# Input quarters of a seven-product projection loaded once and held, four pairs begun before the sums, recurrence units placed earlier

## The chip, the cores and the metric

One Trainium2 chip, one of its cores. The metric is the device time of one execution in microseconds (us); the number that counts is the median over runs. The engines are TensorE (PE in the profile, its weight loads PEld), VectorE (DVE), ScalarE (ACT), GpSimd (POOL) and SyncE (SP), which here only issues loads.

## The reference

A decoder layer over 2048 tokens of width 1024 in float32. One input projection feeds two groups: a gated linear recurrence (HGRN2, four heads of 128) and sliding-window attention with sinks (eight query heads, two key heads). Their gated outputs go through one output projection, and LayerNorm ends the layer:

```python
h = jnp.einsum('btd,de->bte', h_res, w_in[layer])          # 1024 -> 3328 columns
hq, hf, hi, hg, aq, ak, av, ag = jnp.split(h, IN_SPLITS, axis=-1)
f = lb + (1.0 - lb) * jax.nn.sigmoid(hf)
o_h = hgrn2_chunk(silu(hq), 1.0 - f, hi, log(f))           # S_t = diag(f_t) S_{t-1} + (1-f_t) i_t^T
o_h = rms_norm(o_h) * hg_norm_w * silu(hg)
o_a = swa_with_sinks(partial_rope(aq), partial_rope(ak), av, sinks[layer]) * silu(ag)
out = jnp.einsum('btd,de->bte', jnp.concatenate([o_h, o_a], -1), w_out[layer])
z = DN_ALPHA * h_res + out                                  # then LayerNorm with ln_g, ln_b
```

## The kernel before

**Projection.** The 26 column tiles of 128 are taken in 13 pairs (`PAIRS`, L38), the tokens in two super-blocks of 1024. A super-block and a pair make a 2 x 2 block product, which is done with seven products instead of eight. The blocks of x are a11, a12 (first 512 tokens, lower and upper half of the 1024 inputs), a21, a22 (second 512 tokens). Besides a11, a12 and a22 the products use four sums: s1 = a21 + a22, s2 = s1 - a11, s3 = a11 - a21, s4 = a12 - s2. Each of these operands is four tiles of 128 x 512 and is called a quarter here where it is a block of x. The product numbers are those of the weights: 1 (with a11), 2 (a12), 6 (s2), 5 (s1), 7 (s3), 3 (s4), 4 (a22); the weights 4 to 7 are sums, too (t1, t2 in `Weights.make`, L267), made in the first super-block, stored in DRAM (kw) and loaded again in the second.
Every operand is split into a high and a low part, the high one by ScalarE (L184), the low one by VectorE (L185). A product is then 12 matmuls of 512 columns (`product`, L323). Three accumulators hold the results in PSUM: px, py and pz, from a pool `mm_ps` of six banks that attention and recurrence use as well.

**Order.** The 91 products of a super-block are its slots (L761 on). The slots begin with products 1 and 2 of the first `GROUP` pairs, three before the change, because these need no sums; after them each pair's others follow in the order 6, 5, 7, 3, 4. `SuperBlock` (L207) makes the operands: a11 and a12 ahead of the first slot, then `sums` (a21 and a22 loaded, s1, s2, s3), `late` (a12 loaded a second time, s4) and `last` (a22 loaded a second time). The second super-block's are made around slot 91. These second loads, and every weight load, go into one pool of five tiles of 256 KB (`raw_tile`, L153).

**Units.** Attention and recurrence run in pieces between the slots: `attend(j, b)` (L384, seven steps) and `recur(j, b)` (L523, ten steps) for head group j and token block b. The table `units_at` (L777) gives each the slot of its first step and how many slots lie between two steps. Slots past 182 are ticks of the output projection, two for each half of an output tile. Attention queries (qa) and the recurrence's decayed keys and queries (kq) live in a pool of two 1 MB tiles, `q_tile` (L171); decays live in a pool of four e tiles (`e_tile`, L168), where attention has its keys. A recurrence unit multiplies running products of the forget gate (scans L548, L549), a reciprocal (L558) and factors on GpSimd (L560, L561) into kq, transposes the keys on TensorE (kp, L604), and updates a state (L643) for each of four chunks.

**Output projection.** For each of 16 token tiles `out_prepare` (L699) reloads the spilled recurrence and attention outputs (mh, ms), transposes mh, and `out_tile` (L718) does two halves of 24 matmuls (L739 to L741) and the LayerNorm. Its scale lg is kept in two e tiles, its shift lb in the two tmp tiles.

The program is written in this order, and a scheduler places each engine's instructions when the program is built; every engine then runs its own list strictly in order, SP's list of loads included.

Of the kernel before, what the change touches and what calls it, by code (L numbers as in the profile page):

```python
# [10 lines left out]
F32 = mybir.dt.float32  # L11
# [29 lines left out]
GROUP = 3  # L41
# [3 lines left out]
def tile_hybrid_layer(  # L45
# [161 lines left out]
    class SuperBlock:  # L207
# [10 lines left out]

        def a12(self):
            for q in range(4):  # L220
                self.put("a12", q, load_x(self.s, 0, 4 + q, raw_tile, f"r12{q}"))

        def sums(self, q):
            a21, a22 = load_x(self.s, 1, q, t_tile, f"r21{q}"), load_x(self.s, 1, 4 + q, raw_tile, f"p22{q}")
            s1, s2 = raw_tile(f"x{self.s}_s1{q}"), tmp_tile(f"x{self.s}_s2{q}")
            nc.vector.tensor_add(s1, a21, a22)
            nc.vector.tensor_sub(s2, s1, self.r11[q])
            nc.vector.tensor_sub(a21, self.r11[q], a21)
            self.put("s2", q, s2)
# [488 lines left out]
    def out_tile(n, m, made, after):  # L718
        if not lns:
            lg, lbt = [e_tile(f"lg{c}")[:, 0:512] for c in range(2)], [tmp_tile(f"lb{c}") for c in range(2)]  # L720
            for c in range(2):
                nc.sync.dma_start(lg[c], lng[:, c * 512 : (c + 1) * 512].to_broadcast([P, 512]))
                nc.sync.dma_start(lbt[c], lnb[:, c * 512 : (c + 1) * 512].to_broadcast([P, 512]))
            lns.extend([lg, lbt])
# [46 lines left out]
    for g, (s, t, m, w, p) in enumerate(slots):  # L771
# [6 lines left out]
        24: (attend, 0, 0, 3), 38: (attend, 0, 1, 3), 52: (attend, 1, 0, 3), 66: (attend, 1, 1, 3),  # L778
        96: (recur, 0, 0, 2), 106: (recur, 0, 1, 2), 117: (attend, 0, 2, 2), 126: (recur, 1, 0, 2),
        135: (attend, 0, 3, 2), 144: (recur, 1, 1, 2), 153: (attend, 1, 2, 2), 162: (attend, 1, 3, 2),  # L780
# [35 lines left out]
    for g in range(1, LEAD):  # L816
        if g != GROUP:
            make(g)
# [109 lines left out]
```

## Time and profile before

| | |
|---|---|
| median of 3 runs | 1017.3 us (1011.54 to 1021.37) |
| profiled execution, own time | 1012.9 us |
| its span, first to last instruction | 1011.2 us |
| mean granted TensorE clock | 0.939 |
| TensorE busy | 898.4 us (89%) |
| VectorE busy | 644.4 us (64%) |
| ScalarE busy | 462.1 us (46%) |
| GpSimd busy | 268.4 us (27%) |
| moved by DMA | 206.71 MB, mean 204 GB/s |

Busy times are sums over the span of one execution. A matmul's own duration overlaps with the next one's, so the distance between two starts is what one costs. A wait in brackets is idle time of the engine just before an instruction, with the event that ended it. The granted clock is a share of 2.4 GHz.

### The profile page before, as it was taken

To read this page: it belongs to the slowest core of one execution; us is meant where nothing else is said; L and a number is where in the kernel's file an instruction comes from. 1 tells how busy PE (TensorE), PEld (TensorE's weight loads), DVE (VectorE), ACT (ScalarE), POOL (GpSimd) and SP (SyncE) were. 2 spreads that over 40 slices of the span, in tenths; PEclk is the share of its full clock that TensorE was granted. 3 is DMA by queue.
4 is the path that set the end of the run, shared out by engine and by line. 5 is a ranking of instruction groups with operands and counts; after the bars stand their busy time and mean duration, and the time that the engine had idled before them with its cause. 6 is when DMAs were issued, how large, how long until landed. Compare 5 with 4: busy or idle time off the path is not lost.

```text
span 1011.2 us, 14557 instructions
## 1 busy us (share of the span) xinstructions
PE 898.4 (89%) x4542; PEld 714.7 (71%) x4542; DVE 644.4 (64%) x1280; ACT 462.1 (46%) x1236; POOL 268.4 (27%) x444
## 2 busy tenths in 40 slices
PE   8149899999999985899989998999999959699996
PEld 6037687777777764677867886877778747578884
DVE  5956677565665599675556545444886885755554
ACT  5422455444444445365553553554775645433221
POOL 1114333222333102433222222222322222212111
PEclk9669899999999996999999998999999979889998
DMA  6398996767546758778676658556795534234322
GB/s 226 99 308 287 300 330 217 242 211 239 204 177 237 268 188 306 254 252 230 224 209 226 205 185 241 178 141 237 255 311 166 176 101 139 91 110 136 104 84 83
DMA packets 97950, 206.71 MB, mean 204 GB/s; under 512 B 14161, under 2 KB 31697, under 8 KB 97873
## 3 DMA queue, kind: packets, MB, share of 16 engines
q1 hardware_dynamic: 73904, 127.11, 41.2%
q0 software_dynamic: 23680, 78.15, 20.6%
q8 instruction: 36, 0.59, 0.3%
q10 hardware_dynamic: 288, 0.52, 0.1%
q14 instruction: 42, 0.34, 0.1%
HBM read 124.59 MB, written 78.64 MB: 201 GB/s over the span
## 4 chain that ended last, share of the span: by engine, by line
PE 66%; DMA 8%; DVE 7%; ACT 3%; issue 3%; SPq 1%; POOL 1%; DVEq 0%; POOLq 0%; ACTq 0%
PE px L329 7%; PE px L330 7%; PE px L331 7%; PE po L739 5%; PE po L740 5%; PE po L741 5%; PE pz L329 4%; PE pz L331 4%; PE pz L330 4%; PE op L495 2%; DMA r<-proj 2%; PE py L329 2%; PE sp L445 2%; PE py L331 2%; PE py L330 1%
## 5 line engine op out<-in xcount | busy, mean ns | idle before, releaser
L296 POOL DMA_DIRECT2D proj<-s x48 | 26.7, 556 | 141.0 <-DVE s L351 127.6
L346 ACT ACTIVATE s<-px 128x512 f32<-128x512 f32 x52 | 31.0, 597 | 51.3 <-PE px L331 49.2
L558 DVE RECIPROCAL f<-e 128x512 f32<-128x512 f32 x16 | 53.4, 3339 | 0.2
L468 POOL TENSOR_TENSOR wt<-wt,st 128x512 f32<-128x512 f32 x32 | 33.4, 1042 | 56.4 <-DVE st L467 45.5
L459 ACT ACTIVATE wt<-sp,st 128x129 f32<-128x129 f32 x128 | 45.5, 371 | 3.2 <-DVE st L455 2.6
L185 DVE TENSOR_TENSOR w<-w,w 128x512 fp32r<-128x512 f32 x42 | 31.5, 754 | 23.6 <-ACT w L184 23.6
L329 PE MATMUL px<-x_s20h,w 128*128 128x512 f32 x26 | 11.4, 440 | 36.9 <-ACT w L184 35.9
L290 POOL DMA_DIRECT2D kw<-w x52 | 28.2, 543 | 55.7 <-DVE w L185 49.8
L742 DVE SCALAR_TENSOR_TENSOR xr<-xr,po 128x512 f32<-128x512 f32 x32 | 21.9, 683 | 32.7 <-PE po L741 32.5
L454 ACT ACTIVATE sp<-sink 128x2 f32<-128x2 f32 x64 | 11.1, 175 | 66.2 <-DVE st L451 61.6
L753 ACT ACTIVATE xr<-xr,rs 128x512 f32<-128x512 f32 x32 | 24.3, 808 | 33.6 <-DVE rs L750 33.6
L445 PE MATMUL sp<-kh,qa 128*128 128x256 f32 (+1 forms) x128 | 35.3, 301 | 4.2 <-DMA w<-in_wt_dram 2.7
L450 DVE COPY_PREDICATED sp<-past,sp 128x256 f32<-128x256 int32 x60 | 24.9, 422 | 20.4 <-PE sp L446 19.9
L618 ACT ACTIVATE u<-s,e 128x128 f32<-128x128 f32 x60 | 22.0, 399 | 26.5 <-DVE s L643 21.5
L756 POOL DMA_DIRECT2D out_dram<-xr x30 | 17.6, 588 | 57.2 <-DVE xr L755 56.5
L446 PE MATMUL sp<-kl,qa 128*128 128x256 f32 (+1 forms) x128 | 32.8, 286 | 0.0
L329 PEld LDWEIGHTS px<-x_s20h,w 128*128 128x128 f32 x26 | 5.0, 193 | 39.1 <-ACT w L184 36.8
L184 ACT ACTIVATE w<-w 128x512 fp32r<-128x512 f32 x42 | 26.2, 628 | 14.1 <-DMA w_0a<-in_wt_dram 3.7
L445 PEld LDWEIGHTS sp<-kh,qa 128*128 128x128 f32 x128 | 24.5, 191 | 10.2 <-issue 6.8
L185 DVE TENSOR_TENSOR w<-w_0a,w 128x512 fp32r<-128x512 f32 x26 | 19.1, 735 | 18.8 <-ACT w L184 16.8
L184 ACT ACTIVATE w<-w_t 128x512 fp32r<-128x512 f32 x26 | 16.3, 631 | 31.3 <-PE px L331 13.9
L184 ACT ACTIVATE w<-w_1a 128x512 fp32r<-128x512 f32 x36 | 22.8, 633 | 17.1 <-PE py L331 14.6
(513 smaller groups left out, 3201.9 us busy)
## 6 DMA issues: line engine op xcount, KB each, us to landing
kw<-w POOLq DMA_DIRECT2D x52, 512.0 KB, 4.5
w<-kw SPq DMA_DIRECT2D x52, 512.0 KB, 4.9
proj<-s POOLq DMA_DIRECT2D x60, 256.0 KB, 3.9
w<-in_wt_dram SPq DMA_DIRECT2D x45, 256.0 KB, 5.2
x_r<-in_xt_dram SPq DMA_DIRECT2D x32, 256.0 KB, 5.4
r<-proj SPq DMA_DIRECT2D x32, 256.0 KB, 4.5
vg<-proj SPq DMA_DIRECT2D x64, 128.0 KB, 4.2
xr<-in_xn_dram SPq DMA_DIRECT2D x32, 256.0 KB, 3.2
```

Of the source, the lines that this page charges most:

```text
L184: nc.scalar.activation(h, src, AF.Copy)
L185: nc.vector.tensor_sub(l, src, h.bitcast(F32))
L329: nc.tensor.matmul(ps, lhsT=ah, rhs=bh, start=start, stop=False, skip_group_check=not first)
L330: nc.tensor.matmul(ps, lhsT=ah, rhs=bl, start=False, stop=False, skip_group_check=not first)
L331: nc.tensor.matmul(ps, lhsT=al, rhs=bh, start=False, stop=q == 3, skip_group_check=not first)
L445: nc.tensor.matmul(sp[:, h, lo:], lhsT=lhs, rhs=kh[:, kc], start=True, stop=False)
L459: nc.scalar.activation(wt_[:, s, :], sps[s // 2][:, s % 2, P - 1 :], AF.Exp, bias=st[:, 1, s : s + 1], scale=0.125, accum_out=st[:, 2, s : ...
L468: nc.gpsimd.tensor_mul(wt_[:, :, 1:], wt_[:, :, 1:], st[:, 0, :].unsqueeze(2).to_broadcast([P, 4, P]))
L558: nc.vector.reciprocal(re, e[:, :, 1:129])
L739: nc.tensor.matmul(ps, lhsT=h[:, q], rhs=wh, start=e == 0, stop=False)
L740: nc.tensor.matmul(ps, lhsT=h[:, q], rhs=wl, start=False, stop=False)
L741: nc.tensor.matmul(ps, lhsT=l[:, q], rhs=wh, start=False, stop=e == 7)
```

## The change

Each quarter of x is loaded once for a super-block: a12 and a22 go into the two tiles of `q_tile`, in two loads of 512 KB each, and stay there; a21 is held in four t tiles. s4 is then made in place, in the order a12 - s2 by one subtraction of the unsplit s2 instead of two of its parts. `GROUP` is 4: pair (6, 7) joins the pairs that begin with products 1 and 2. s3, s4 and the split of a22 are written at slot 3 of the super-block (`late`). The LayerNorm's scale and shift move into two tiles of the weight pool `w`. In the table of units the four attention units of the first super-block begin at slots 23, 33, 43 and 53 with two slots a step (before: 24, 38, 52 and 66 with three), recur(0, 0) begins at 66 (before 96), the others follow from 97 on, and recur(1, 2) and (1, 3) begin at 186 and 200 with three slots a step (before 191 and 201 with two). So two recurrence units begin beside the output projection, as before, but those before them, (0, 2) and (0, 3), start 8 and 9 slots earlier.

```diff
-GROUP = 3
+GROUP = 4
...
+        def held(self, half, name):
+            t = q_tile(f"x{self.s}_{name}")
+            for k2 in range(2):
+                nc.sync.dma_start(
+                    t[:, 2 * k2 : 2 * k2 + 2],
+                    xt[2 * self.s + half, 2 + k2].rearrange("p (k t) -> p k t", t=TB),
+                )
+            return [t[:, q] for q in range(4)]
+
         def a12(self):
+            self.r12 = self.held(0, "r12")
             for q in range(4):
-                self.put("a12", q, load_x(self.s, 0, 4 + q, raw_tile, f"r12{q}"))
+                self.put("a12", q, self.r12[q])
+
+        def fetch(self):
+            self.r21 = [load_x(self.s, 1, q, t_tile, f"r21{q}") for q in range(4)]
+            self.r22 = self.held(1, "r22")
 
         def sums(self, q):
-            a21, a22 = load_x(self.s, 1, q, t_tile, f"r21{q}"), load_x(self.s, 1, 4 + q, raw_tile, f"p22{q}")
-            s1, s2 = raw_tile(f"x{self.s}_s1{q}"), tmp_tile(f"x{self.s}_s2{q}")
+            a21, a22 = self.r21[q], self.r22[q]
+            s1, s2 = tmp_tile(f"x{self.s}_s1{q}"), tmp_tile(f"x{self.s}_s2{q}")
             nc.vector.tensor_add(s1, a21, a22)
             nc.vector.tensor_sub(s2, s1, self.r11[q])
-            nc.vector.tensor_sub(a21, self.r11[q], a21)
             self.put("s2", q, s2)
+            nc.vector.tensor_sub(self.r12[q], self.r12[q], s2)
             self.put("s1", q, s1)
-            self.put("s3", q, a21)
-
-        def late(self, q):
-            a12 = load_x(self.s, 0, 4 + q, raw_tile, f"p12{q}")
-            h, l = self.made["s2"][q]
-            nc.vector.tensor_sub(a12, a12, h.bitcast(F32))
-            nc.vector.tensor_sub(a12, a12, l.bitcast(F32))
-            self.put("s4", q, a12)
-
-        def last(self, q):
-            self.put("a22", q, load_x(self.s, 1, 4 + q, raw_tile, f"r22{q}"))
+
+        def late(self):
+            for q in range(4):
+                nc.vector.tensor_sub(self.r21[q], self.r11[q], self.r21[q])
+                self.put("s3", q, self.r21[q])
+            for q in range(4):
+                self.put("s4", q, self.r12[q])
+            for q in range(4):
+                self.put("a22", q, self.r22[q])
...
-            lg, lbt = [e_tile(f"lg{c}")[:, 0:512] for c in range(2)], [tmp_tile(f"lb{c}") for c in range(2)]
...
+            both = [ring.tile([P, 2, 512], F32, tag="w", name=f"ln{c}", bufs=5) for c in range(2)]
...
-        96: (recur, 0, 0, 2), 106: (recur, 0, 1, 2), 117: (attend, 0, 2, 2), 126: (recur, 1, 0, 2),
...
+        66: (recur, 0, 0, 2),
...
+        if g == 0:
+            for q in range(4):
+                sb0.sums(q)
+        elif g == 3:
+            sb0.late()
...
         if g == NS - 7:
             sb1.a11()
         elif g == NS - 6:
             sb1.a12()
+            sb1.fetch()
         elif g == NS - 1:
             for q in range(4):
                 sb1.sums(q)
-            for q in range(4):
-                sb1.late(q)
-            for q in range(4):
-                sb1.last(q)
...
+        elif g == NS + 2:
+            sb1.late()
```

Three places of the built order follow, first as it was, then as it is.

VectorE in the first super-block, around the weight sums t1 and t2 of the first pair (w0_0_t1, w0_0_t2), which the first s2 product needs; x0_s43l and x0_a221l to x0_a223l are low parts of s4 and a22, w0_0_0, w0_5_0 and w0_5_1 raw weights. Before:

```order
L185 TENSOR_TENSOR x0_s43l_537<-x0_p123_532,x0_s43h_536 128x512
L185 TENSOR_TENSOR x0_a221l_549<-x0_r221_546,x0_a221h_548 128x512
L185 TENSOR_TENSOR x0_a222l_555<-x0_r222_552,x0_a222h_554 128x512
L185 TENSOR_TENSOR x0_a223l_561<-x0_r223_558,x0_a223h_560 128x512
L278 TENSOR_TENSOR w0_0_t1_608<-w0_5_0_604,w0_0_0_600 128x512
L279 TENSOR_TENSOR w0_0_t2_609<-w0_5_1_606,w0_0_t1_608 128x512
L285 TENSOR_TENSOR w0_5_0_604<-w0_5_1_606,w0_5_0_604 128x512
L288 TENSOR_TENSOR w0_0_1_602<-w0_0_1_602,w0_0_t2_609 128x512
L185 TENSOR_TENSOR w0_0_6_612<-w0_0_t2_609,w0_0_6_612 128x512
```

After:

```order
L244 TENSOR_TENSOR x0_r12_407<-x0_r12_407,x0_s23_477 128x512
L185 TENSOR_TENSOR x0_s23l_481<-x0_s23_477,x0_s23h_480 128x512
L291 TENSOR_TENSOR w0_0_t1_618<-w0_5_0_614,w0_0_0_610 128x512
L185 TENSOR_TENSOR x0_s33l_557<-x0_r213_432,x0_s33h_556 128x512
L185 TENSOR_TENSOR x0_s43l_573<-x0_r12_407,x0_s43h_572 128x512
L292 TENSOR_TENSOR w0_0_t2_619<-w0_5_1_616,w0_0_t1_618 128x512
L298 TENSOR_TENSOR w0_5_0_614<-w0_5_1_616,w0_5_0_614 128x512
L301 TENSOR_TENSOR w0_0_1_612<-w0_0_1_612,w0_0_t2_619 128x512
L185 TENSOR_TENSOR w0_0_6_622<-w0_0_t2_619,w0_0_6_622 128x512
```

The splits of a22 stood right ahead of the weight sums and now stand some forty instructions earlier; the last parts of s2, s3 and s4 take their place.

SP's loads at the second super-block (x1_r11 to x1_r22 are quarters of x, x1_p12 and x1_p22 the loads of a quarter that is loaded twice, w1 weights, kw stored weight sums, lb the LayerNorm's shift). Before:

```order
L204 DMA x1_p223_3478<-in_xt_dram 128x512
L274 DMA w1_0_7_3640<-kw0_7_226 128x1024
L204 DMA x1_p120_3497<-in_xt_dram 128x512
L204 DMA x1_p121_3505<-in_xt_dram 128x512
L204 DMA x1_p122_3513<-in_xt_dram 128x512
L204 DMA x1_p123_3521<-in_xt_dram 128x512
L723 DMA lb0_7356<-in_lnb_dram 128x512
L204 DMA x1_r220_3529<-in_xt_dram 128x512
L723 DMA lb1_7357<-in_lnb_dram 128x512
L204 DMA x1_r221_3535<-in_xt_dram 128x512
L204 DMA x1_r222_3541<-in_xt_dram 128x512
```

After:

```order
L259 DMA w1_1_0a_3390<-in_wt_dram 128x512
L223 DMA x1_r22_3534<-in_xt_dram 128x1024
L204 DMA x1_r210_3526<-in_xt_dram 128x512
L204 DMA x1_r211_3528<-in_xt_dram 128x512
L204 DMA x1_r212_3530<-in_xt_dram 128x512
L259 DMA w1_1_1a_3392<-in_wt_dram 128x512
L223 DMA x1_r22_3534<-in_xt_dram 128x1024
L204 DMA x1_r213_3532<-in_xt_dram 128x512
```

The quarters came last, each a second time, between the weights that they share the raw pool with; now a21 and a22 come once, before the weights of the third pair.

VectorE in the output projection, from a state update of recur(0, 3) (s, from hkv0_3_3) to the decays of recur(1, 2) (e2_2, e3_2; xr and po are the projection's). Before:

```order
L742 SCALAR_TENSOR_TENSOR xr4_0_8093<-xr4_0_8093,po4_0_8098 128x512
L643 SCALAR_TENSOR_TENSOR s0_0_4020<-hkv0_3_3_8125,e0_3_7317,ue0_0_3_3_8054 128x128
L643 SCALAR_TENSOR_TENSOR s0_1_4022<-hkv0_3_3_8125,e1_3_7434,ue0_1_3_3_8058 128x128
L743 BN_STATS bst4_8097<-xr4_0_8093 128x6
L548 SCALAR_TENSOR_TENSOR e2_2_7797<-f2_2_7804 128x64
L549 SCALAR_TENSOR_TENSOR e2_2_7797<-f2_2_7804 128x64
```

After:

```order
L562 SCALAR_TENSOR_TENSOR e3_2_7784<-f3_2_7791 128x64
L755 SCALAR_TENSOR_TENSOR xr1_1_7646<-xr1_1_7646,po1_1_7731 128x512
L656 SCALAR_TENSOR_TENSOR s0_0_3162<-hkv0_3_2_7759,e0_3_6996,ue0_0_3_2_7590 128x128
L656 SCALAR_TENSOR_TENSOR s0_1_3164<-hkv0_3_2_7759,e1_3_7087,ue0_1_3_2_7594 128x128
L579 TENSOR_TENSOR kq1_2_7712<-r20_2_7717,f2_2_7720 128x4x64
L725 TENSOR_TENSOR m3_0l_7828<-mp3_7822,m3_0h_7827 128x512
L571 RECIPROCAL f3_2_7791<-e3_2_7784 128x512
L756 BN_STATS bst1_7648<-xr1_1_7646 128x6
L725 TENSOR_TENSOR m7_1l_8383<-ms7_8368,m7_1h_8382 128x512
L755 SCALAR_TENSOR_TENSOR xr2_0_7835<-xr2_0_7835,po2_0_7840 128x512
L656 SCALAR_TENSOR_TENSOR s0_0_3162<-hkv0_3_3_7867,e0_3_6996,ue0_0_3_3_7770 128x128
L656 SCALAR_TENSOR_TENSOR s0_1_3164<-hkv0_3_3_7867,e1_3_7087,ue0_1_3_3_7774 128x128
```

The scans of recur(1, 2) stood behind the last state update of recur(0, 3); now its second reciprocal is done ahead of that update.

## Rows read from the trace of the kernel before

**Rows 1.** TensorE in the page's 40 equal slices of the span, tenths busy
```profile
PE   8149899999999985899989998999999959699996
```

**Rows 2.** Waits of TensorE: line <- releaser: us in total, times, longest
```profile
PE px L329 <- ACT w L184: 40.5, 3, 34.7
PE kp L604 <- POOL kq L561: 16.2, 5, 5.2
...
PE vg L586 <- DMA vg<-proj: 5.3, 3, 2.0
```

**Rows 3.** TensorE's timeline: start us, us, engine, line, operation [idle before <-releaser]
```profile
27.61 0.39 PE L330 MATMUL py<-x_a123l,w 128*128 128x512 f32 x1
27.84 0.39 PE L331 MATMUL py<-x_a123h,w 128*128 128x512 f32 x1
62.91 0.79 PE L329 MATMUL px<-x_s20h,w 128*128 128x512 f32 x1 [34.68 <-ACT w L184]
...
105.34 0.79 PE L329 MATMUL px<-x_a110h,w 128*128 128x512 f32 x1 [4.54 <-ACT w L184]
...
394.13 0.79 PE L329 MATMUL pz<-x_s40h,w 128*128 128x512 f32 x1 [6.83 <-ACT w L184]
...
851.12 0.39 PE L648 MATMUL ho<-u,kq 128*128 128x128 f32 x2
...
882.50 0.48 PE L604 MATMUL kp<-ident,kq 128*128 128x128 f32 x1 [5.25 <-POOL kq L561]
```

**Rows 4.** Stretches: length, busy us of PE, PEld, DVE, ACT, POOL, clock, DMA, GB/s
```profile
0.00:13.00 13.00, 9.32 (x42) 7.67 (x43) 5.66 (x14) 5.70 (x8) 4.80 (x18) 0.94 0.80 259
28.00:63.00 35.00, 0.32 (x2) 0.10 (x1) 28.21 (x47) 11.75 (x21) 4.83 (x7) 0.56 0.54 170
150.00:200.00 50.00, 50.00 (x256) 39.32 (x256) 33.05 (x72) 25.89 (x77) 15.21 (x25) 1.00 0.71 242
368.00:402.00 34.00, 18.38 (x52) 12.12 (x51) 32.17 (x60) 15.71 (x27) 8.06 (x10) 0.70 0.67 241
402.00:700.00 298.00, 280.36 (x1520) 224.16 (x1519) 167.64 (x363) 145.50 (x462) 86.96 (x130) 0.96 0.69 217
823.00:836.00 13.00, 4.12 (x14) 2.30 (x15) 12.31 (x22) 4.10 (x13) 4.88 (x6) 0.53 0.30 94
874.00:888.00 14.00, 3.99 (x21) 2.37 (x20) 14.00 (x31) 6.24 (x22) 6.04 (x11) 0.66 0.13 37
```

**Rows 5.** VectorE's timeline at the start
```profile
23.07 0.68 DVE L226 TENSOR_TENSOR x_s<-x_r,x_p 128x512 f32<-128x512 f32 x1
...
60.43 0.69 DVE L278 TENSOR_TENSOR w_t<-w,w 128x512 f32<-128x512 f32 x1 [3.75 <-DMA w<-in_wt_dram]
61.50 0.69 DVE L279 TENSOR_TENSOR w_t<-w,w_t 128x512 f32<-128x512 f32 x1 [0.38 <-DMA w<-in_wt_dram]
```

**Rows 6.** The queue of SP: issues of loads at the start and in the projection
```profile
25.71 9.95 SPq L204 DMA_DIRECT2D x_p<-in_xt_dram  x5
...
53.76 1.72 SPq L246 DMA_DIRECT2D w<-in_wt_dram  x3
...
860.19 0.80 SPq L703 DMA_DIRECT2D mh<-hg_spill  x2
```

**Rows 7.** ScalarE's timeline before the first weight of pair (6, 7)
```profile
103.66 0.63 ACT L184 ACTIVATE h<-c 128x512 fp32r<-128x512 f32 x1 [4.97 <-DVE c L313]
```

**Rows 8.** GpSimd's timeline in the projection
```profile
874.11 0.10 POOL L538 MEMSET e<- 128x4 f32 x1 [7.70 <-DVE s L643]
```

**Rows 9.** The costliest groups: line, engine, operation | busy us, mean ns | idle before
```profile
L558 DVE RECIPROCAL f<-e 128x512 f32<-128x512 f32 x16 | 53.4, 3339 | 0.2
```

**Rows 10.** Tile mh, a projection tile's recurrence input: time from DMA issue to landing
```profile
DMA to landing us min/median/max: 2.0/2.8/4.7
```

**Rows 11.** DMA issues: count, KB each, median us to landing
```profile
w<-kw SPq DMA_DIRECT2D x52, 512.0 KB, 4.9
...
x_r<-in_xt_dram SPq DMA_DIRECT2D x32, 256.0 KB, 5.4
```

More of the change, by code (lines that the diff above doesn't have):

```diff
@@ L719, in out_tile @@
         if not lns:
-            lg, lbt = [e_tile(f"lg{c}")[:, 0:512] for c in range(2)], [tmp_tile(f"lb{c}") for c in range(2)]
-            for c in range(2):
-                nc.sync.dma_start(lg[c], lng[:, c * 512 : (c + 1) * 512].to_broadcast([P, 512]))
-                nc.sync.dma_start(lbt[c], lnb[:, c * 512 : (c + 1) * 512].to_broadcast([P, 512]))
+            both = [ring.tile([P, 2, 512], F32, tag="w", name=f"ln{c}", bufs=5) for c in range(2)]
+            for t, src in zip(both, (lng, lnb)):
+                nc.sync.dma_start(t, src.rearrange("o (c t) -> o c t", t=512).to_broadcast([P, 2, 512]))
+            lg, lbt = ([t[:, c] for c in range(2)] for t in both)
             lns.extend([lg, lbt])
@@ L807, in tile_hybrid_layer @@
     made_o = units()
-    for w, part in loads.pop(0):
-        if part == 0 and w.pair == PAIRS[0]:
-            w.load(0)
+    first = loads.pop(0)
+    for w, part in first:
+        w.load(part)
+        if w.pair == PAIRS[0] and part == 0:
             make(0)
@@ L813, in tile_hybrid_layer @@
             make(GROUP)
-        else:
-            w.load(part)
     for g in range(1, LEAD):
-        if g != GROUP:
-            make(g)
+        make(g)
     sb0.a12()
-    for q in range(4):
-        sb0.sums(q)
-    for q in range(4):
-        sb0.late(q)
-    for q in range(4):
-        sb0.last(q)
+    sb0.fetch()
     for g, (s, t, m, w, p) in enumerate(slots):
@@ L828, in tile_hybrid_layer @@
             w_.load(part)
-        if g + LEAD != GROUP or LEAD > GROUP:
-            if g + LEAD < len(slots) and slots[g + LEAD][2] not in slots[g + LEAD][3].w:
-                make(g + LEAD)
+        if g == 0:
[3 more added lines that the diff above has]
+            sb0.late()
+        if g + LEAD < len(slots) and slots[g + LEAD][2] not in slots[g + LEAD][3].w:
+            make(g + LEAD)
         p.step(m)
@@ L839, in tile_hybrid_layer @@
                 sb1.sums(q)
-            for q in range(4):
-                sb1.late(q)
-            for q in range(4):
-                sb1.last(q)
-        if g == 2 * NS - 7:
-            load_wo(0, made_o), load_wo(1, made_o)
-        elif g == 2 * NS - 6:
-            load_wo(2, made_o), load_wo(3, made_o)
-        elif g == 2 * NS - 5:
-            load_wo(4, made_o), load_wo(5, made_o)
-        elif g == 2 * NS - 4:
-            load_wo(6, made_o), load_wo(7, made_o)
+        elif g == NS + 2:
+            sb1.late()
+        if 2 * NS - 7 <= g < 2 * NS - 3:
+            e = 2 * (g - (2 * NS - 7))
+            load_wo(e, made_o), load_wo(e + 1, made_o)
         elif g == 2 * NS - 1:
```

7 lines of the change are left out of this document (4 added, 3 removed).

## The prediction

> **What bounds the kernel now.** I read the slices of the span first. TensorE is busy nine tenths or more of nearly every slice; the holes are the second and third slice, the sixteenth, and the 33rd and 35th (25.3 us each) [rows 1]. So TensorE's own work bounds most of the kernel, and the question is which holes the change closes. The list of TensorE's waits names them: 40.5 us for a split weight on ScalarE, nearly all in one wait; 16.2 us for the recurrence's key factors from GpSimd; 5.3 us for loads of its values and gates [rows 2]. TensorE's timeline puts them in place [rows 3]. At the start its last cheap product is issued at 27.84 and the next matmul, on s2, at 62.91. Busy matmuls follow each other every 0.227 us. The stretches of time then show what the other engines do in each hole [rows 4]. From 28 to 63 VectorE is busy 28.21 of 35 us with 47 instructions, 0.60 us each. From 368 to 402, where the second super-block begins, TensorE is busy 18.4 of 34 us, VectorE 32.2, and the granted clock averages 0.70. The two holes in the output projection (823 to 836 and 874 to 888) have VectorE at 12.3 of 13 and 14.0 of 14 us. In all four VectorE is the engine that TensorE ends up waiting for, itself or through ScalarE and GpSimd. From 402 to 700 TensorE stands 17.6 us in small pieces that the change doesn't aim at.
>
> **The start.** The removed part is the second load of a12 and a22. Before, the queue on SP issues these reloads from 25.71 on, each held until one of five raw buffers is free, and the weights of the first s2 product stand behind them, at 53.76 [rows 6]. VectorE's timeline shows the price: its first sum at 23.07, then weight sum t1 at 60.43 after 3.75 us of waiting for a load, t2 at 61.50 [rows 5]. TensorE goes on 1.4 us after t2 starts (split on ScalarE, then the matmul).
> After, there is one load for each quarter, and the weights follow at once. VectorE's first sum needs the first half of a22, whose load ends with the 22nd block of 256 KB. By 13 us the DMAs have moved 259 GB/s x 13 us = 3.4 MB [rows 4], 12.8 such blocks; 9.2 more at that rate take 9.3 us, so it lands at about 22 us. I take 23.1, the time of the first sum before, with bounds 21 and 26. From the first sum to t2 VectorE now issues 49 instructions, so t2 starts at 23.1 + 48 x 0.60 = 51.9 and TensorE goes on at 53.3, not 62.9: 9.6 us. Two more products (24 matmuls x 0.227 = 5.4 us, pair (6, 7)) have been done by then, under the same cover: TensorE's cheap work ends at 33.5, still 20 us before. Gain 15.0 us; the bounds of the first sum, and 2 us of waits between h and l splits, give 10 to 17. VectorE is what is late next, so the hole shrinks and stays.
> The Trainium skill ("Perfetto Trace Analysis", DMA Optimizations) says that splitting DMAs into smaller pieces may let some work start sooner, which speaks against joining two 256 KB loads into one of 512 KB. By that rule the first sum waits for one block more, 1.0 us at 259 GB/s, and the gain would be 14.0. In the list of issues the 512 KB loads land no later than those of 256 KB (4.9 against 5.4 us) [rows 11], so by the row it costs nothing. The sum keeps 15.0.
> A side hole goes with it in part. At 105.34 TensorE stands 4.54 us for the first weight of pair (6, 7) [rows 3]: ScalarE, in order, had sat 4.97 us on the split of a rotated tile whose sum was late [rows 7]. That pair now begins some 85 us earlier, among the first products, but the same split now stands ahead of its weight 6. Between 0 and 4.5 us, I take 2.3.
>
> **The second super-block.** Before, the 34 us hold 52 TensorE instructions, nearly all of them matmuls of these products, which back to back at 0.227 take 11.8; so 22.2 us are lost, 15.6 of them idle and the rest at the lower of the clock's two levels (0.70 of 2.4 GHz on average) [rows 4]. The longest piece, 6.83 us before 394.13, is ScalarE's split of a weight [rows 3]. After, a12 and a22 of the second super-block are loaded once, a12 before the last pair begins, and no raw buffer holds them back. What holds a22 back is recur(0, 0), which now runs in slots 66 to 84. In the changed order TensorE has 178 matmuls (40.4 us) between that recurrence's last read of its q4 buffer, which frees it for a22, and the last matmul of the first s2 product. In that time a22 must land (5.4 us, the time to landing in rows 11) and VectorE issue 50 instructions (30.0 us at 0.60): 35.4 us, so 5 us are to spare and the hole closes. Against it: with four open pairs three px accumulators besides pz stay in the six PSUM banks when recur(0, 1) comes to its scores, one more than before, and its transposes may wait for a bank. No row shows that wait; the nearest is the idle time in small pieces from 402 on, 17.6 us in 298 with recurrences in most of them [rows 4], so 0 to 9 us, half of it. Most of those pieces are loads and in-order splits, not banks, so I take 2 and count 20, bounds 8 and 22.
>
> **The middle.** Attention units in the first super-block come every 10 slots, not every 14, and recur(0, 0) joins. From 150 to 200 VectorE is busy 33.05 of 50 us [rows 4], in which about 14 slots and one unit pass. Four slots fewer are 10.9 us of TensorE and some 5 us of VectorE: 28 of 39 us, 0.72. TensorE covers that, so I count nothing. The 17.6 us of idle between 402 and 700 have one recurrence fewer to come from, but their order is new: nothing, bounds -9 and +9. The eight subtractions of a12 that go (8 x 0.60 = 4.8 us of VectorE) lie within the two holes and are in the counts above. The 4.2 MB of loads saved cost no one once the holes are closed; two more weight loads lie under the first products.
>
> **The output projection.** Before, the LayerNorm scale takes two of the four e buffers, so a recurrence unit's decay tiles wait until the unit before has done its last state update: the memset of e stands 7.70 us for it at 874.11 [rows 8]. Then 16 scans, two reciprocals of 3.3 us [rows 9] and the factors come in one run, and TensorE, in order, stands at the transposes of the keys (5.25 us before 882.50 [rows 3]). With the scale and shift in the weight ring, the changed order has the reciprocals before that update, so these waits go: 16.2 + 5.3 = 21.5 us [rows 2]. Each hole is followed by some six matmuls at half the clock, 2.5 us in two. New is that recur(1, 2) and (1, 3) are spread over three ticks a step and end nearer to the tiles that read them. From the last matmul of an output half at 851.12 [rows 3] to the issue of its reload at 860.19 [rows 6] and its landing 2.8 us later [rows 10] are 11.9 us. TensorE has about 12.6 us of other work in that place for the tightest tile (two halves of 24 matmuls and a transposition group). So 0 to 4 us may come back; I take 2. Gain 21.5 + 2.5 - 2 = 22, bounds 12 and 24.
>
> **Sum.** 15.0 + 2.3 + 20 + 22 = 59.3 us. The profiled execution took 1012.9 us (span 1011.2), so 953.6 by its own time. The median of the runs shown is 1017.3, 4.4 above it, so I forecast 958 for the median. With the bounds of all terms the gain lies between 21 and 77, but not all fall short together; the forecast's own range is 945 to 971.
>
> **Rivals.**
> The start doesn't move: the first sum comes late, or VectorE is held by the h splits, and t2 stays at 61 us. For it: after the change VectorE has as many instructions ahead of t2 as it had. Against: from 23.07 to 61.50 are 38.4 us, and some 50 instructions fill only 30.0 of them; 8.4 were waits, for reloads. Price 10 to 15: 970.
> The second super-block's hole moves instead of closing. The two held quarters take both q4 buffers, so the loads of a22 wait for recur(0, 0), and everything behind them on SP waits too; that the change doesn't do there what it says. For it: only 5 us to spare. Against: the loads are issued in the same place where TensorE still has a whole pair. Price 20: 978.
> The projection's waits return as waits for the spilled recurrence output. For it: 11.9 against 12.6 us. Against: only two tiles are that tight. Price 22: 980.
> Slower: VectorE becomes the bound in slots 23 to 65, where units now come every 10 slots. At 32.2 of 34 us of VectorE TensorE lost 15.6 idle of 34 [rows 4]; over 43 slots x 2.72 = 117 us that would be 54 us, and the quarter of the second super-block, behind recur(0, 0), would lose its 20 too: 958 + 74 = 1032. It decides from about nine tenths of VectorE on; my estimate of 0.72 is well below.
>
> **How the numbers follow.** Forecast 0.60; start 0.10; second super-block 0.14; projection 0.10; slower 0.04; 0.02 for several of these together, near no change. For 8 in 10 the range reaches over the three middle cases, with a little room below for gaps of the middle that close too: 938 to 988. A measurement tells about 1% (10 us) from no change here. Every case but the last two is faster by more: faster 0.94, same 0.02, slower 0.04.
>
> **What would show it.** In the changed profile: TensorE's first wait should be some 20 us and end near 53; the second hole should be gone, with no granted clock below 0.9 in that stretch; the list of TensorE's waits should lack the key transposes on GpSimd; VectorE at some 0.72 in the first super-block with TensorE full. I am wrong if the s2 product still starts after 58, if a new wait above 5 us stands at the second super-block's first products, or if TensorE waits for the output's transposes.

## The result, and the profile after

The changed kernel takes 957.99 us in the median of 4 runs (955.72 to 964.3), the kernel before 1016.21 beside it (4 runs, 1011.54 to 1021.37). The ratio is 0.9436, with a 95% interval of 0.937 to 0.9502: 58 us faster. The forecast was 958. The profiled execution takes 956.75 us (span 955.0, mean granted clock 0.971) where that of before took 1012.91 (span 1011.2, 0.939), so 56.2 us are to be explained.

The page's slices of TensorE and its granted clock, changed kernel:

```profile
PE   8478999999999999869999999989998999999995
PEclk9879999999999999979999999999999999999998
```

Of the holes in [rows 1] the pair at the start is narrower and those in the output projection are gone. The one of the second super-block, the sixteenth slice before, is shallower and lies two slices on. TensorE's list of waits (line, releaser, us in total, times, longest) says the same:

```profile
PE px L342 <- ACT w L184: 23.8, 2, 19.8
PE sp L458 <- DMA qa<-hl: 5.6, 2, 3.9
PE px L342 <- DMA w<-kw: 4.7, 2, 4.4
PE pz L342 <- ACT s L359: 4.3, 2, 3.1
PE ho L659 <- ACT om L674: 2.7, 1, 2.7
```

The waits for the key factors (kp from GpSimd, 16.2 us) and for vg (5.3 us) of [rows 2] are missing; the split weight went from 40.5 to 23.8 us. To compare stages I cut both spans where the first s2 product starts and where the first output matmul starts. TensorE alone, kernel before (stretch, length, busy us with count, clock, DMA share, GB/s):

```profile
0.00:62.91 62.91, 24.55 (x105) 0.73 0.60 195
62.91:749.75 686.84, 644.36 (x3242) 0.96 0.71 235
749.75:1011.20 261.45, 229.48 (x1196) 0.94 0.39 125
```

The same for the changed kernel:

```profile
0.00:54.84 54.84, 30.68 (x128) 0.83 0.64 212
54.84:730.41 675.57, 644.83 (x3313) 0.98 0.72 239
730.41:955.00 224.59, 214.63 (x1102) 0.98 0.41 134
```

Length less busy time is TensorE's idle time: 38.4, 42.5 and 32.0 us before; 24.2, 30.7 and 10.0 after. That is 14.2, 11.7 and 22.0 us less, 47.9 in all. The other 8.3 us are busy time (898.4 to 890.1): the same matmuls, fewer of them at the lower clock. These three idle sums serve for all runs below.

In the changed kernel's stretches (length, busy us of PE, PEld, DVE, ACT, POOL, clock, DMA, GB/s) the holes look so:

```profile
28.00:54.80 26.80, 6.32 (x27) 4.58 (x25) 26.80 (x46) 10.85 (x19) 5.66 (x9) 0.71 0.43 133
150.00:200.00 50.00, 49.78 (x264) 36.59 (x263) 33.67 (x80) 24.53 (x80) 15.66 (x26) 1.00 0.78 237
330.00:402.00 72.00, 68.66 (x307) 55.80 (x306) 57.59 (x102) 41.07 (x85) 15.75 (x26) 1.00 0.72 251
402.00:430.00 28.00, 19.58 (x87) 15.32 (x86) 14.96 (x28) 7.97 (x17) 12.95 (x19) 0.76 0.74 252
```

Beside [rows 4]: at the start VectorE is now busy without a gap (26.80 of 26.80 us). From 330 to 402, where the second super-block begins, TensorE loses 3.3 us. But the 28 us after that hold 8.4 us of idle time, with VectorE only half busy. TensorE's timeline puts the holes in place:

```profile
34.64 0.39 PE L344 MATMUL py<-x_a123h,w 128*128 128x512 f32 x1
54.84 0.80 PE L342 MATMUL px<-x_s20h,w 128*128 128x512 f32 x1 [19.82 <-ACT w L184]
...
94.22 0.80 PE L342 MATMUL px<-x_s20h,w 128*128 128x512 f32 x1 [4.02 <-ACT w L184]
...
405.30 0.66 PE L617 MATMUL kp<-ident,kq 128*128 128x128 f32 x4 [0.88 <-ACT kt L622]
409.07 0.79 PE L342 MATMUL pz<-x_s40h,w 128*128 128x512 f32 x1 [3.12 <-ACT s L359]
...
423.90 0.80 PE L342 MATMUL px<-x_s20h,w 128*128 128x512 f32 x1 [4.43 <-DMA w<-kw]
```

And VectorE's timeline at the start, against [rows 5]: first sum, a wait, weight sums t1 and t2.

```profile
22.22 0.68 DVE L241 TENSOR_TENSOR x_s<-x_r,x_r 128x512 f32<-128x512 f32 x1
24.33 0.69 DVE L185 TENSOR_TENSOR x_a220l<-x_r,x_a220h 128x512 fp32r<-128x512 f32 x1 [1.43 <-ACT x_a220h L184]
...
51.65 0.67 DVE L291 TENSOR_TENSOR w_t<-w,w 128x512 f32<-128x512 f32 x1
...
53.45 0.67 DVE L292 TENSOR_TENSOR w_t<-w,w_t 128x512 f32<-128x512 f32 x1
```

### The profile page after: what moved, and what is told of

Read it like the earlier page. It is cut to its first block, busy times and chain, and to the rows that moved or that the text cites. A ratio compares the mean times of both kernels' runs of the same rounds, so it can differ in the third digit from the quotient of the medians.

```text
span 955.0 us, 14480 instructions
## 1 busy us (share of the span) xinstructions
PE 890.1 (93%) x4542; PEld 708.8 (74%) x4542; DVE 634.7 (66%) x1272; ACT 460.8 (48%) x1236; POOL 270.4 (28%) x444
## 4 chain that ended last, share of the span: by engine, by line
PE 70%; DMA 13%; DVE 9%; issue 3%; SPq 3%; ACT 2%; POOL 0%; DVEq 0%; POOLq 0%; ACTq 0%
PE px L342 7%; PE px L343 7%; PE px L344 7%; PE po L752 6%; PE po L753 6%; PE po L754 6%; PE pz L342 4%; PE pz L343 4%; PE pz L344 4%; DMA w<-in_wt_dram 3%; PE op L508 3%; DMA w<-kw 2%; PE sp L458 1%; PE sp L459 1%; PE hkv L647 1%
## 5 line engine op out<-in xcount | busy, mean ns | idle before, releaser
L481 POOL TENSOR_TENSOR wt<-wt,st 128x512 f32<-128x512 f32 x32 | 34.0, 1062 | 62.1 <-DVE st L480 59.3
L467 ACT ACTIVATE sp<-sink 128x2 f32<-128x2 f32 x64 | 11.1, 176 | 62.7 <-DVE st L464 59.1
L303 POOL DMA_DIRECT2D kw<-w x52 | 28.5, 547 | 39.7 <-DVE w L185 36.8
L342 PE MATMUL px<-x_s20h,w 128*128 128x512 f32 x26 | 12.2, 469 | 28.5 <-ACT w L184 23.8
L518 POOL DMA_DIRECT2D sw_spill<-mix x32 | 17.9, 561 | 63.6 <-DVE mix L517 51.8
L631 ACT ACTIVATE u<-s,e 128x128 f32<-128x128 f32 x60 | 21.4, 396 | 27.3 <-DVE s L656 22.9
L493 ACT ACTIVATE pall<-pt 128x512 f32<-128x512 f32 x32 | 19.1, 596 | 30.1 <-PE pt L490 29.4
L517 DVE TENSOR_TENSOR mix<-op,gate 128x128 f32<-128x128 f32 x64 | 15.4, 282 | 26.9 <-PE op L508 26.1
L458 PEld LDWEIGHTS sp<-kh,qa 128*128 128x128 f32 x128 | 24.4, 193 | 11.8 <-DMA qa<-hl 7.9
L359 ACT ACTIVATE c<-px 128x512 f32<-128x512 f32 x26 | 15.6, 600 | 29.3 <-PE px L344 24.7
```

What stands on the lines that cost most here:

```text
L342: nc.tensor.matmul(ps, lhsT=ah, rhs=bh, start=start, stop=False, skip_group_check=not first)
L359: nc.scalar.activation(t, ps, AF.Copy)
L458: nc.tensor.matmul(sp[:, h, lo:], lhsT=lhs, rhs=kh[:, kc], start=True, stop=False)
L481: nc.gpsimd.tensor_mul(wt_[:, :, 1:], wt_[:, :, 1:], st[:, 0, :].unsqueeze(2).to_broadcast([P, 4, P]))
```

## The experiments

Four edits are in the change: the single load of each quarter ("load"), the fourth open pair ("pair"), the table of units ("units") and the LayerNorm's scale and shift in the weight pool ("LN"). Eight runs take one or two of them alone, leave one out, or undo a part of one; four try what the traces suggested. The pair and the table were not run alone on the kernel before. Ratios are to runs of the kernel before beside each (medians 1013.5 to 1016.2). Idle is TensorE's, in the three stretches above (to the first s2 product, to the first output matmul, to the end).

| kernel | median us | ratio to before, 95% interval | idle us |
|---|---|---|---|
| before | 1016 | 1 | 38.4, 42.5, 32.0 |
| LN alone | 991.4 | 0.9766 (0.9727 to 0.9805) | 39.0, 44.5, 9.8 |
| load alone | 992.6 | 0.9798 (0.9764 to 0.9832) | 27.2, 37.0, 33.0 |
| load and LN | 967.0 | 0.9522 (0.9485 to 0.956) | 27.3, 35.9, 9.8 |
| all but pair | 970.1 | 0.9577 (0.9519 to 0.9634) | 26.4, 40.6, 10.2 |
| all but units | 965.4 | 0.952 (0.9479 to 0.9561) | 23.0, 40.1, 9.6 |
| all but LN (last two units as before) | 974.7 | 0.9595 (0.9549 to 0.9641) | 23.6, 35.4, 19.5 |
| all but load | 1007.4 | 0.9936 (0.9902 to 0.997) | 36.8, 56.6, 9.7 |
| all, last two units as before | 958.1 | 0.9445 (0.9394 to 0.9495) | 23.6, 33.8, 10.0 |
| all four: the change | 958.0 | 0.9436 (0.937 to 0.9502) | 24.2, 30.7, 10.0 |

### The output projection: e buffers or spread

Does the projection gain because the scale leaves the e buffers, or because the last two units are spread over three ticks? Three kernels tell. The changed kernel with the spread undone:

```diff
-        172: (recur, 0, 3, 2), 186: (recur, 1, 2, 3), 200: (recur, 1, 3, 3),
+        172: (recur, 0, 3, 2), 191: (recur, 1, 2, 2), 201: (recur, 1, 3, 2),
```

> The changed kernel with the last two recurrence units at slots 191 and 201, two slots a step, as they stood before the change (LayerNorm's scale and shift stay in the weight pool). Theory E, the two e buffers that the scale gave back closed the projection's holes: the new spread adds nothing, 956 to 963 us, and TensorE has no wait for the key factors above 2 us in the projection. Rival S, the spread over three slots closed them: both holes return, 973 to 983 us, some 16 us of waits for the key factors (kq) and 5 us for vg.

It took 958.14 us. The same with the LayerNorm's tiles put back as well:

```diff
-            both = [ring.tile([P, 2, 512], F32, tag="w", name=f"ln{c}", bufs=5) for c in range(2)]
...
+            lg, lbt = [e_tile(f"lg{c}")[:, 0:512] for c in range(2)], [tmp_tile(f"lb{c}") for c in range(2)]
```

> The changed kernel with the LayerNorm's scale and shift back in two e tiles and the two tmp tiles, and the last two units at 191 and 201 with two slots a step (so against the run with only these two slots moved it differs by the place of the scale and shift alone). Theory E: the memset of e waits some 7 us for the last state update again, and the time is 16 to 26 us above that of the run with only the slots moved, 974 to 985 us. Rival S: it is within 4 us of that run.

It took 974.69 us, 16.6 above. And the kernel before with these lines the other way round, its only edit:

> The kernel before with one edit, the LayerNorm's scale and shift in two tiles of the weight pool. Theory E: the waits for the key factors (16.2 us) and for vg (5.3 us) go, with some clock time: 992 to 1000 us against 1016, ratio 0.976 to 0.984. Rival S: no change, ratio 0.996 to 1.004.

It took 991.43 us, 24.8 less than before and 0.6 under theory E's range in time, with the ratio inside it. Theory E holds, S falls: the spread does nothing. The edit moves scale and shift together, but the shift's two tmp tiles are used by nothing else in the projection (in the changed kernel L240 and L290 alone take one), so what counts is the e tiles. The projection's idle time goes from 32.0 to 9.8 us with the LN edit alone. In the kernel with the tiles put back, GpSimd's memset of e waits again for a state update, and 8 us later TensorE for the key factors (GpSimd's and TensorE's timelines):

```profile
838.10 0.11 POOL L551 MEMSET e<- 128x4 f32 x1 [7.45 <-DVE s L656]
...
846.43 0.48 PE L617 MATMUL kp<-ident,kq 128*128 128x128 f32 x1 [5.30 <-POOL kq L574]
```

That is [rows 8] and the last row of [rows 3] once more. With the new table there is one such hole and not two, which is why the edit is worth 16.6 us there and 24.8 in the kernel before.

### The single load

The load alone (three pairs, old units, LN back):

> The single load alone: the changed kernel with three open pairs, the whole table of units as before, and the LayerNorm's scale and shift in e and tmp tiles again, so that against the kernel before only the loads, the sums and their place differ. Theory H, the start's wait and the second super-block's hole both close by the load alone and the projection's holes (some 20 us) stay: 985 to 998 us. Rival I, the load pays only together with four open pairs and the moved units: 1002 to 1016 us.

It took 992.59 us, ratio 0.9798: theory H. The s2 product starts at 51.06, 11.9 us earlier, and the start's idle time falls by 11.1 us. VectorE's first sum comes at 20.83, 2.2 us earlier than before; from there to t2 it waits 6.8 us less (nothing, where it had waited 6.8) and executes four instructions fewer (some 2.4 us). So the edit gains by its loads and, less, by the shorter list. In the second super-block TensorE's row of this run is:

```profile
330.00:430.00 100.00, 88.59 (x412) 0.93 0.71 241
```

That is 11.4 us of idle time in these 100 us, as in the changed kernel (11.8), where the kernel before has 19.7. Units and slots are those of before, so the same work can be timed as well: from the first s2 product there to that of the fourth pair it is 74.0 us (357.16 to 431.13) instead of 87.9 (367.92 to 455.80). The load alone is worth 13.9 us there, with the clock. The other way round, the changed kernel with the second loads put back:

```diff
-            self.r12 = self.held(0, "r12")
             for q in range(4):
-                self.put("a12", q, self.r12[q])
+                self.put("a12", q, load_x(self.s, 0, 4 + q, raw_tile, f"r12{q}"))
...
-            a21, a22 = self.r21[q], self.r22[q]
+            a21, a22 = load_x(self.s, 1, q, t_tile, f"r21{q}"), load_x(self.s, 1, 4 + q, raw_tile, f"p22{q}")
```

> The changed kernel with a12 and a22 loaded twice into the raw pool again, and sums, late and last written where they stood before (four open pairs, the new units and the LayerNorm's place stay). Theory H, the single load is what moves the start and closes the second super-block's hole: the first s2 product starts at 60 to 66 us instead of 54.8, an idle stretch of 8 us or more comes back between 330 and 402, and the time is 970 to 990 us. Rival U, units and open pairs did most of it: the s2 product starts below 58 and the time is 956 to 966 us.

It took 1007.36 us: the direction of theory H, but 17 us beyond its range. The load is worth 21 us on its own and 49 with the other three edits in place. The s2 product comes even later than its 60 to 66 us. TensorE's and VectorE's timelines at its start:

```profile
67.83 0.80 PE L330 MATMUL px<-x_s20h,w 128*128 128x512 f32 x1 [31.46 <-ACT w L184]
```

```profile
65.01 0.69 DVE L279 TENSOR_TENSOR w_t<-w,w 128x512 f32<-128x512 f32 x1 [4.55 <-DMA w<-in_wt_dram]
```

VectorE waits 4.55 us for a weight queued behind the reloads, as it waited 3.75 in [rows 5]. The idle time up to the first output matmul is 56.6 us, more than the 42.5 of the kernel before; from 330 to 402 it is 4.3, so the stretch of 8 us that theory H named there does not come back in that place; a wait of 6.39 us stands behind it, at 409.93. A reason that fits is that the earlier units and the fourth pair add transfers and tiles to the place where the reloads already held the queue; no run shows it apart. What is shown is that the fourth pair and the new table together cost time without the single load.

### The fourth pair and the units

Three open pairs in the changed kernel:

```diff
-GROUP = 4
+GROUP = 3
```

> The changed kernel with three open pairs at the start instead of four. Theory C, the fourth pair's two cheap products are 5.4 us of work under the start's wait: TensorE's cheap work ends 5.4 us earlier, the s2 product still starts at 54 to 56, and the time is 962 to 968 us. Rival B, the fourth pair's accumulators held back the recurrence beside the second super-block (the idle pieces from 402 to 424, 8.4 us): these pieces shrink and the time stays at 954 to 960 us.

It took 970.14 us, somewhat above theory C's range, and not for its reason. Rival B falls: from 402 to 430 TensorE idles 11.1 us, not less than with four pairs (8.4). VectorE and TensorE at its start:

```profile
19.47 0.69 DVE L241 TENSOR_TENSOR x_s<-x_r,x_r 128x512 f32<-128x512 f32 x1 [1.02 <-DMA x_r<-in_xt_dram]
...
48.31 0.68 DVE L292 TENSOR_TENSOR w_t<-w,w_t 128x512 f32<-128x512 f32 x1
```

```profile
49.70 0.79 PE L342 MATMUL px<-x_s20h,w 128*128 128x512 f32 x1 [23.57 <-ACT w L184]
```

SP's issue of the two loads of a22, with three pairs and then with four:

```profile
12.24 1.00 SPq L223 DMA_DIRECT2D x_r<-in_xt_dram  x2
```

```profile
14.52 1.61 SPq L223 DMA_DIRECT2D x_r<-in_xt_dram  x2
```

Without the fourth pair the first sum runs 2.75 us earlier and the s2 product 5.1 us earlier, with 5.4 us less work done by then: there is next to nothing between them. The first sum accounts for half of the 5.1: a22 is issued 2.3 us earlier. The rest lies between the first sum and t2. With four pairs VectorE waits 1.43 us there (24.33) for a split of a22 on ScalarE, which stands in order behind the copy of the fourth pair's own accumulator, and it executes two instructions more (1.2 us). That copy on ScalarE:

```profile
23.18 0.60 ACT L359 ACTIVATE s<-px 128x512 f32<-128x512 f32 x1 [1.60 <-PE px L344]
```

Over all runs with the single load, but for the one that fetches a22 earlier (below), the start's idle time is 26.4 to 27.3 us with three pairs and 23.0 to 24.2 with four. So the pair is worth about 3 us there, not 5.4. The other 10 us of this kernel lie in the middle (40.6 against 30.7 us idle); its longest waits there are 7.4 us for vg and 5.5 for qa.

The old table of units in the changed kernel:

> The changed kernel with the whole table of units as it was before (recur(0, 0) at 96 again, attention every 14 slots). Theory H, the single load alone closes the second super-block's hole: the time is 956 to 964 us and TensorE idles under 8 us from 330 to 402. Rival U, moving recur(0, 0) away from the sums was needed: VectorE is full from slot 91 on, TensorE idles 10 us or more there, and the time is 966 to 980 us.

It took 965.39 us, between the two theories: 7 us for the table, though the intervals overlap. The place is theory H's: from 330 to 402 TensorE idles 7.1 us. So the table's gain lies elsewhere. The stretch to the first output matmul idles 40.1 us, the projection 9.6. One wait of it is for the first output tile's spilled recurrence output:

```profile
727.32 1.27 PE L719 MATMUL mp<-ident,mh 128*128 128x128 f32 x4 [2.87 <-DMA mh<-hg_spill]
```

It stands in the two other runs with the LN edit and the whole old table as well (3.1 us with LN alone, 3.0 with load and LN), and in none with the new table above 0.5.

The load and the LN edit together, without pair and units:

> The single load and the LayerNorm's new place together: the changed kernel with three open pairs and the whole table of units as before. Theory A, what the edits gave alone (ratios 0.9798 and 0.9766) multiplies: 0.957, or 968 to 974 us, and the fourth pair and the moved units are worth the last 10 to 16 us only together, since either alone left 965 to 970. Rival F, the fourth pair is worth 5 us or more without the moved units, or the two edits overlap: 975 us or more.

It took 966.98 us, a little under theory A's range (0.9522 where 0.957 was expected); F falls. The fourth pair on top of it gives 965.4, the units 970.1, which the intervals do not tell from 967. Both together give 958; its interval, too, overlaps with two of theirs, but the run with all four edits and only the last two units as before gives 958.1 again. Each alone loses in the middle what the other avoids: 35.9 us idle with neither, 40.1 and 40.6 with one, 30.7 with both. The waits that make it up are of a few us each, at different places in each kernel (a rotated tile, a load of qa, of vg, of a stored weight). Which collision it is that the pair removes from the new table is open.

Five open pairs:

```diff
-GROUP = 4
+GROUP = 5
```

> The changed kernel with five open pairs at the start. Theory C, two more products (5.4 us) lie under the start's wait: the s2 product starts at most 3 us later than at 54.8 and the time is 951 to 956 us. Rival B, as from three to four pairs the loads of a22 move back by what the work gains, and five px accumulators and pz hold all six PSUM banks, so that units beside the open pairs wait: 960 to 975 us.

It took 974.94 us: the time of rival B, though the s2 product starts at 57.25, 2.4 us later, as theory C had it. TensorE idles only 15.7 us up to there, but loses more later (49.9 us to the first output matmul). Its timeline:

```profile
34.69 0.47 PE L342 MATMUL py<-x_a120h,w 128*128 128x512 f32 x1 [1.81 <-DVE s L364]
...
54.44 0.47 PE L342 MATMUL py<-x_a120h,w 128*128 128x512 f32 x1 [1.46 <-DVE s L364]
...
430.09 0.47 PE L613 MATMUL ap<-kq 128*64 128x128 f32 x1 [12.31 <-DVE hg L603]
```

Four cheap products (py) now wait for an accumulator that VectorE reads out between its sums, and in the second super-block one recurrence step stands 12.31 us before its scores (ap). VectorE at that place:

```profile
425.21 0.69 DVE L325 TENSOR_TENSOR c<-c,cs 128x512 f32<-128x512 f32 x1 [4.58 <-DMA hl<-h]
427.57 0.69 DVE L326 TENSOR_TENSOR c<-c,sw 128x512 f32<-128x512 f32 x1 [1.67 <-POOL sw L324]
...
429.62 0.91 DVE L603 SCALAR_TENSOR_TENSOR hg<-hg,vg 128x256 f32<-128x256 f32 x2
```

The scores don't use vg; what they share with it is the pool of six PSUM banks. So the bank is what TensorE waits for, as rival B had it: it comes free when VectorE has read vg (L603). That read stands on VectorE behind a rotated tile that waits for its own transfers, so a late load is passed on to work that has nothing to do with it.

### Attempts at the holes that are left

The parts of s3, s4 and a22 written later, so that the weight sums could go ahead of them:

```diff
-        elif g == 3:
-            sb0.late()
...
+        if 6 <= g < 9:
+            sb0.late(g - 6)
```

> The changed kernel with the parts of s3, s4 and a22 in the first super-block written at slots 6, 7 and 8, behind the making of the first weight sums, instead of all at slot 3. Theory V, the start is a queue of VectorE instructions: 16 of them (9.6 us at 0.60) move behind weight sum t2, the s2 product starts at 45 to 50 us, and of that 3 to 9 us remain at the end: 948 to 955 us. Rival W, the first pair's products 7, 3 and 4 then wait for the same instructions, so that the idle time only moves to a later place of the start: 956 to 961 us.

It took 956.18 us (ratio 0.9435, 0.9401 to 0.9469): no difference. But it tells neither theory from the other, since the scheduler built VectorE's list up to t2 in the changed kernel's order; the parts of the last s3 and s4 stand between t1 and t2 as they did. VectorE's timeline of this run, t1 and t2:

```profile
50.40 0.68 DVE L294 TENSOR_TENSOR w_t<-w,w 128x512 f32<-128x512 f32 x1
...
52.20 0.68 DVE L295 TENSOR_TENSOR w_t<-w,w_t 128x512 f32<-128x512 f32 x1
```

One reason that fits: t1 and t2 take the two tmp tiles, which s1 and s2 of the last quarter hold until they are split. That was not tried.

a22 fetched earlier, ahead of the third and fourth pair's weights:

```diff
+        elif w.pair == PAIRS[1] and part == 0:
+            sb0.fetch()
...
     sb0.a12()
-    sb0.fetch()
```

> The changed kernel with a21 and a22 of the first super-block fetched behind the weights of the second pair, ahead of those of the third and fourth and of a12. Theory V, the start is VectorE's queue behind the first sum, so an earlier a22 starts it earlier: first sum at 16 to 18 us instead of 22.2, the s2 product at 50 to 53 instead of 54.8, 952 to 956 us. Rival W, TensorE's cheap products wait for the weights and a12 instead and VectorE has the same work ahead of t2: the s2 product at 54 or later, 957 to 963 us.

It took 959.86 us: the places of theory V, the time of W. First sum and TensorE:

```profile
15.94 0.69 DVE L241 TENSOR_TENSOR x_s<-x_r,x_r 128x512 f32<-128x512 f32 x1 [1.65 <-DMA x_r<-in_xt_dram]
```

```profile
19.94 0.79 PE L342 MATMUL px<-x_a110h,w 128*128 128x512 f32 x1 [4.32 <-ACT w L184]
...
52.81 0.80 PE L342 MATMUL px<-x_s20h,w 128*128 128x512 f32 x1 [12.27 <-ACT w L184]
```

The first sum is 6.3 us earlier, the s2 product 2.0, because the splits of a12 and of the weights, which had come ahead of the sums, now stand between them. And TensorE waits 4.32 us for a cheap product's weight. VectorE's amount of work, more than the arrival of a22, is what holds the start.

The units behind the rotated tiles moved by a few slots:

```diff
-        97: (recur, 0, 1, 2), 107: (recur, 1, 0, 2), 118: (attend, 0, 2, 2), 126: (attend, 0, 3, 2),
+        101: (recur, 0, 1, 2), 111: (recur, 1, 0, 2), 120: (attend, 0, 2, 2), 130: (attend, 0, 3, 2),
```

> The changed kernel with recur(0, 1), recur(1, 0) and the two attention units behind them begun at slots 101, 111, 120 and 130 instead of 97, 107, 118 and 126. Theory R, the idle 8.4 us from 402 to 424 come from that recurrence's instructions standing ahead of the rotated tile's on ScalarE, VectorE and GpSimd: moved away from them they shrink below 4 us, 950 to 956 us. Rival M, these instructions meet another late tile wherever they stand: as much idle time at another place, 956 to 964 us.

It took 960.15 us: rival M; from 402 to 430 TensorE still idles 7.9 us. The wait before s4's product shrank from 3.12 to 1.21 us, but TensorE's timeline has the wait for a stored weight still, 10 us earlier:

```profile
413.36 0.80 PE L342 MATMUL px<-x_s20h,w 128*128 128x512 f32 x1 [5.07 <-DMA w<-kw]
```

The idle time to the first output matmul is 32.3 us, against 30.7. None of these versions beats the changed kernel by more than its interval.

## Why the prediction was right, and where its parts were not

The gain was forecast at 59.3 us and is 56.2 between the profiled executions. The three large holes were the right ones, and each shrank by the edits that were named for it; single terms missed, the second super-block's most. That the median came out at the forecast to the decimal is luck: the sum put the profiled execution at 953.6, 3.2 us below its 956.75, and the 4.4 us added for the median were 1.2. None of the three signs of being wrong came. One thing that was to show the mechanism failed: a clock nowhere below 0.9 at the second hole holds up to 402 (1.00) and not behind it (0.76).

**The start: 15.0 forecast, 14.2 less idle time.** VectorE was the bound as the step said: the first sum came at 22.22 (23.1), t2 at 53.45 (51.9), TensorE went on at 54.84 (53.3). From the first sum to t2 it is 2.4 us longer than worked out: the wait of 1.43 for a split on ScalarE and 0.8 of a slower VectorE operation (last section). Joining the loads of a22 cost nothing here: the first sum follows the instruction ahead of it without a wait. What failed is that the fourth pair's products lie "under the same cover" and its weight loads under the first products. The pair's loads move the issue of a22 back by 2.3 us, and its copies and sums stand in the lists of ScalarE and VectorE ahead of t2. The load alone gave 11.1, where 9.6 had been worked out for it; the pair about 3, not 5.4. Two misses of opposite sign made the term right.

**The side hole: 2.3 forecast, 0.5 found** (4.54 us in [rows 3], 4.02 at 94.22 after), near the lower bound. The split of a rotated tile stands ahead of the weight on ScalarE again (4.29 us), but the weight itself comes late, too. VectorE's t1 and t2 of this pair in the changed kernel:

```profile
91.07 0.69 DVE L291 TENSOR_TENSOR w_t<-w,w 128x512 f32<-128x512 f32 x1 [3.19 <-DMA w<-in_wt_dram]
...
92.81 0.69 DVE L292 TENSOR_TENSOR w_t<-w,w_t 128x512 f32<-128x512 f32 x1 [0.44 <-DMA w<-in_wt_dram]
```

The weight sum itself waits for a raw weight's load. In the kernel before, too, t1 waits for such a load (3.81 us at 101.73), and the rotated tile's sum, for which ScalarE sits, is behind it on VectorE. So a late load is behind the wait both times, and no edit brings it forward.

**The second super-block: 20 forecast.** From 330 to 402 the hole closed as worked out, clock and all: 15.6 us of idle time before, 3.3 after, and the clock at 1.00. Only half of it is a gain, since the 28 us behind idle 8.4 us, where the kernel before had 4.1. Its row for the same stretch, TensorE alone:

```profile
402.00:430.00 28.00, 23.91 (x120) 0.96 0.75 258
```

So 8.0 us of idle time went, not 15.6 less 2. The 20 had 6.6 us for the clock in it. That part can't be read off alone here, but the load alone gave 13.9 us in this place with the clock, so the term was some 6 too large. The step that failed is the cost of the recurrence beside the open pairs, set at 2 us for a PSUM bank. No wait for one of the six banks stands there; the transposes wait 0.88 us, for the one tile that they have to themselves (`tr_ps`, L83). The waits are of another kind: the copy of pz out of PSUM that s4's product needs (3.12) and a stored weight (4.43). ScalarE at that copy:

```profile
408.42 0.60 ACT L359 ACTIVATE s<-pz 128x512 f32<-128x512 f32 x1 [1.20 <-DMA vals<-s]
```

The product that pz holds was done at 398, ten microseconds earlier. The copy stands behind a weight's split and the recurrence's copies on ScalarE, and then waits for its buffer, which by the profile a tile's store to DRAM still read. The rival that this hole moves instead of closing described half of the case. Its reason, loads that wait for recur(0, 0), doesn't show.

**The middle: 0 forecast.** All idle time between the first s2 product and the first output matmul fell by 11.7 us, side hole and second super-block included; 0.5 and 8.0 of it are these two. The rest, 3.2, lies well within the bounds of 9. VectorE did not become the bound: from 150 to 200 it is busy 33.67 of 50 us, 0.67, where 0.72 was estimated, with TensorE full. The slower rival falls by its own measure.

**The projection: 22 forecast, some 24.** Idle time fell by 22.0 us against 21.5, and the edit alone gave 24.8 with the clock. The term "2 may come back" found nothing in the changed kernel: no wait for the spilled output appears, with the last units spread or not. The 2.9 to 3.1 us in the runs with the whole old table are before the first output tile, not at the tight one that the step had in mind.

**What the sum could not show.** Terms were added as if each edit had its own. The runs show that LN and load add up within the intervals (0.9766 times 0.9798 is 0.957; 0.9522 measured), but that the pair and the units are worth 9 us only together, and together below nothing without the load: LN alone is 991.4, LN with pair and units 1007.4.

## What to carry to other kernels

Look for what is loaded a second time, and for what holds a buffer through a stage without being part of its rotation: here a reload blocked a queue for everything behind it (21 us alone), and a scale parked in two of four rotating buffers cost 25. Independent work put under a wait is worth its time less what it pushes back itself, so count the bytes that it sends ahead of the load that ends the wait, and its instructions on the engines that end it. Edits to an order are not additive: test them with and without the edit that makes room for them.

## What the runs showed of the hardware

A VectorE operation with both inputs in SBUF took more than twice as long at the start where GpSimd was busy with a product of its own. The changed kernel, GpSimd then VectorE:

```profile
33.64 1.29 POOL L324 TENSOR_TENSOR sw<-sw,cs 128x512 f32<-128x512 f32 x1 [26.04 <-DVE sw L323]
```

```profile
33.98 1.49 DVE L242 TENSOR_TENSOR x_s<-x_s,x_r 128x512 f32<-128x512 f32 x1
35.40 0.68 DVE L249 TENSOR_TENSOR x_r<-x_r,x_r 128x512 f32<-128x512 f32 x1
```

With three pairs the same pair of engines meets at another operation, GpSimd's at 30.03 for 1.56 us and VectorE's (L249) at 30.38 for 1.75 instead of 0.68. In both, VectorE's operation ends 0.54 us after GpSimd's, as if it had begun only then. The Trainium skill ("SBUF — State Buffer", SBUF: two separate sides) says that a VectorE operation with two SBUF inputs and a GpSimd operation that reads SBUF lock each other out for a whole instruction; both rows agree. It cost 0.8 us here, and it speaks against handing the s3 subtractions to GpSimd, which was not run.
